# Lookup gates with one product per token: high and low part as 256 moving columns, added outside, rows accessed in pairs of words

## The chip, the cores and the metric

The kernel runs on one core of a Trainium2 chip. Its engines work side by side, each through its own queue of instructions: TensorE (PE, with its loads of the stationary operand shown as PEld), VectorE (DVE), ScalarE (ACT), GpSimd (POOL) and SyncE (SP), which issues the DMAs. The metric is the device time of one execution in microseconds; lower is better.

## What is computed

256 tokens of width 1024 pass two layers and then a second block (band attention, a recurrence, a mixture of experts, a gated output). Each of the two layers has a mixer and then this lookup of experts, and the change lies in the lookup alone:

```python
def peer(xn, w_q, sub_keys, u, v):          # 8 heads, 128 keys, 16 picks
    q = (t @ w_q).reshape(n_tok, PEER_HEADS, 2, PEER_DKEY // 2)
    sc = jnp.einsum('thpd,hpnd->thpn', q, sub_keys)
    s1, i1 = lax.top_k(sc[:, :, 0], PEER_TOPK)
    s2, i2 = lax.top_k(sc[:, :, 1], PEER_TOPK)
    cand = s1[..., :, None] + s2[..., None, :]     # of 256, the best 16
    cidx = i1[..., :, None] * PEER_NKEYS + i2[..., None, :]
    ...
    gate = jax.nn.softmax(top_s, axis=-1)
    hid = gelu(einsum('td,thkd->thk', tc, u[ec]))
    return einsum('thk,thkd->td', gc * hid, v[ec])
```

There are 128 x 128 = 16384 experts, and each token picks 8 x 16 = 128 of them.

## The kernel before

The kernel gathers no expert. It computes the hidden value of all 16384 experts for all 256 tokens and multiplies each by a gate, which is zero where the token did not pick that expert. The hidden values lie in `H`, by row: expert number = 128 * i1 + i2, `H` has i2 on its 128 partitions, and for each of the 128 rows i1 the 256 tokens side by side in float32. `H` is three tiles, `parts`: rows 0 to 63, 64 to 95, 96 to 127.

One layer of `peer` goes through these stages.

1. Queries (16 blocks) and the scores against the keys.
2. The row stage. For each row i1, `acc_t` (all its products carry the line of `mm`, L119) makes 24 products of 256 columns into the PSUM tile `ph`: 8 blocks of the width, each as high x high, low x high (alternating) and then 8 times high x low. The stationary operand is the row's weight block. It comes by DMA as `raw`, ACT casts its high part `whi`, DVE subtracts for the low part `wlo` (both L98). ACT takes the Gelu of `ph` (L771 for tokens whose gates are not yet in `H`, L774 for the others), and DVE multiplies the latter into the row (L775).
3. Beside the first 28 or so rows DVE chooses the experts (top 16, lookups). From then on, it also makes the gates, 4 tokens at a time in 64 groups, which `rate` spreads evenly over the remaining rows. `build` makes two one-hot tiles in float16: `pab` says at which of 128 places each of the 128 picks of a token has its i1 and its i2 (L735), `pgb` is the i2 half times the pick's gate (L738), once by the high and once by the low float16 part of the gate. `gates` sums over the picks on PE and lets the result meet `H`: rows that are already done (n of them) are multiplied on DVE (L755), the rows to come get the gate written into `H` by ACT (L758), and the Gelu is multiplied into it later.
4. The value stage, `acc`: rows of `H` in pairs are split into `hw`, ACT first and then DVE, and multiplied with the value weights by products of 512 columns. When a token half is finished, L824 adds it to `h`.

The gates of before are two products for each token, one by each part, which add up in PSUM:

```python
mm(ps[:, i * P:(i + 1) * P], b[:, part, :, i], ab[:, 0, :, i], part == 0, part == 1)
```

So 8 products of 128 columns for a group, each with its own stationary operand. In `pab` and `pgb` the 4 tokens lie side by side, so that one token's operand is one element in 4. The sum of a group is a PSUM bank of 512 words, [4 tokens][128 rows]. PSUM tiles of the small kind come from `smt` (4 buffers of one bank). `H` is accessed through `"p i t -> p t i"`: rows run fastest, which are 256 words apart, so no two words in a row of the access lie side by side.

Of the kernel before, what the change touches and what calls it, by code (L numbers as in the profile page):

```python
# [32 lines left out]
# pairs (a, b) of sorted candidates that can be among the best 16: first a, rows, columns  # L33
RECTS = ((0, 2, 16), (2, 2, 8), (4, 4, 4), (8, 8, 2))
NCAND = 80
# gates are held as two float16 parts of 2 ** 14 times their value
GATE_UNIT = 2.0 ** 14
# (1 + w) ** -0.5 - 1 as a polynomial in w, from the first power on
SQRT = (-0.49999831, 0.37499936, -0.3139437, 0.27433988)
NO_SYNC = mybir.DependencyInfo(mybir.DependencyClass.NoSync, mybir.DependencyReason.DATA)  # L40
# products of other work between two steps of the triangular inverses
PACE = 5
# pairs of expert rows for which the first token tile goes ahead of the second
TAIL = 2
# pieces of the first expert's weights split ahead of the choice of experts
EARLY = 2
# output gates of the recurrence that go ahead of the attention's projection
GATES = 0
REST = 2
# loads under way beside the usual ones while the experts' weights stream  # L50
# [3 lines left out]
def program(tc, A, out, stop=None, start=None):  # L54
# [18 lines left out]
    sm_ps = ctx.enter_context(tc.tile_pool(name="sm_ps", bufs=4, space=PSUM))  # L73
# [7 lines left out]
    def smt(nm="sm"):  # L81
        return sm_ps.tile([P, 512], F32, tag="sm", name=nm)
# [34 lines left out]
    def mm(o, l, r, start, stop):  # L117
        """a product; while paced, every few of them queue behind the next mark."""
        i = nc.tensor.matmul(o, l, r, start=start, stop=stop)  # L119
        per, n = paced  # L120
        if per and n // per < len(marks):
            tc.add_manual_dep(i.ins, marks[n // per].name, NO_SYNC, reason="pace")
            paced[1] += 1
        return i
# [6 lines left out]
    def acc_t(o, w, xT, base, nk, n=P):  # L131
        """o[n, t] = sum over nk blocks of w[:, base + k * P ...].T @ xT[:, k, :], high parts first."""
        for a, bs in ((0, (0, 1)), (1, (0,))):
            for k in range(nk):
                ws = w[a][:, base + k * P:base + k * P + n]
                for b in bs:
                    mm(o, ws, xT[b][:, k, :], a == 0 and b == 0 and k == 0, a == 1 and k == nk - 1)
# [20 lines left out]
    def rsqrt(r, v):  # L158
        """r = v ** -0.5: a first guess y from the exponent, then r = y * (1 + w) ** -0.5 with w = v * y ** 2 - 1,
        |w| < 0.07, whose polynomial is off by 2.4e-8 at most."""  # L160
# [37 lines left out]
    def to_T1(src, emit):  # L198
        """src[128, 1024] transposed block by block: emit(q, psum[128, 512]) for blocks 4 q to 4 q + 3."""
        for q in range(2):  # L200
            ps = smt("tp")
            for j in range(4):
                k = 4 * q + j
                nc.tensor.transpose(ps[:, j * P:(j + 1) * P], src[:, k * P:(k + 1) * P], ident)  # L204
            emit(q, ps.rearrange("p (k t) -> p k t", k=4))
# [7 lines left out]
    class Scratch:  # L213
        """room for a norm: half rows that come and go, and rows that stay."""
# [10 lines left out]
    class Rms:  # L225
        """rms norm of h with gain gi, token tile by token tile, into the transposed high and low parts."""
# [39 lines left out]
    class Unscaled(Rms):  # L266
        """the same without the token's scale, which late() returns beside it."""
# [16 lines left out]
    class Ln:  # L284
        """layer norm of the rows y, with the gain's and the bias's rows gb, into h and its transposed
        high and low parts, or to the output."""
# [40 lines left out]
    class Entry(Ln):  # L327
        """final rms norm of the first block and the layer norm that opens the second, in one."""
# [14 lines left out]
        def variance(self, t, v, var):  # L343
            # the rows lack the rms norm's scale, which divides the layer norm's epsilon instead
            q = tinyp.tile([P, 1], F32, tag="rv1", name="rv1")
            V.tensor_tensor(q, self.ss[:, t, 0:1], self.ss[:, t, 1:2], op=ALU.add)
            V.tensor_scalar(q, q, 1e-5 / D, 1e-11, op0=ALU.mult, op1=ALU.add)
            V.tensor_tensor(v, var, q, op=ALU.add)
# [10 lines left out]
    def fresh(make):  # L359
        """the norm of h as it stands."""  # L360
        with pool("fresh") as fp:
            nxt = make(Scratch(fp))
            for t in range(2):
                for n in range(2):
                    nxt.half(t, n)
            return nxt.late()

    def out_proj(wpool, src, xT, sink, order=(0, 1, 2, 3), both=1):
        """x @ w for w [1024, 1024], its granules in this order.
        After the first ones the first token tile goes ahead of the second."""  # L370
# [192 lines left out]
    def peer(l, xT, make):  # L563
        with ExitStack() as es:
# [10 lines left out]
            # routing scratch lies in the half of the hidden values that is written last  # L575
# [138 lines left out]

            w = wload(A["peer_w_q"][l, 0])
# [16 lines left out]
            def build(grp):  # L732
                ts = slice(4 * grp, 4 * grp + 4)
# [3 lines left out]
                b = pw.tile([P, 2, P, 4], F16, tag="pgb", name="pgb", bufs=2)  # L737
                V.tensor_tensor(b, ab[:, 1:2, :, :].to_broadcast([P, 2, P, 4]),  # L738
                                IT[:, 2:4, ts][:, :, None, :].to_broadcast([P, 2, P, 4]), op=ALU.mult)
                built[grp] = ab, b  # L740

            def gates(grp, n):
                t0 = 4 * grp
                ab, b = built.pop(grp)
                ps = smt("g")
                for i in range(4):
                    for part in range(2):
                        mm(ps[:, i * P:(i + 1) * P], b[:, part, :, i], ab[:, 0, :, i], part == 0, part == 1)
                pv = ps.rearrange("p (t i) -> p t i", t=4)
                for o, end, part in parts:  # L750
                    size = end - o
                    hv = part[:, :, t0:t0 + 4].rearrange("p i t -> p t i")
                    m = min(max(n - o, 0), size)
                    if m:
                        V.scalar_tensor_tensor(hv[:, :, :m], hv[:, :, :m], 1.0 / GATE_UNIT, pv[:, :, o:o + m],  # L755
                                               op0=ALU.mult, op1=ALU.mult)
                    if m < size:
                        ACT.activation(hv[:, :, m:], pv[:, :, o + m:end], AF.Copy, scale=1.0 / GATE_UNIT)  # L758
# [30 lines left out]
            while grp < 64:  # L789
                if grp not in built:  # L790
                    build(grp)
                gates(grp, NK)
                grp += 1
            acc = [[mmt(f"acc{t}{n}") for n in range(2)] for t in range(2)]
# [24 lines left out]
            # the last ones for the first token tile, then for the second  # L819
            for t in range(2):  # L820
                for n in range(2):
                    for i1, w, v in held:
                        value_block(i1, w, v, t, (n,))
                    V.tensor_tensor(h[:, t, half(n)], h[:, t, half(n)], acc[t][n], op=ALU.add)  # L824
# [16 lines left out]
    def residual(y, ln):  # L841
        """alpha * h plus a product, into the layer norm."""
# [8 lines left out]
    def band_mixer(xT):  # L851
        """alpha * x + mixed, then its layer norm."""
# [23 lines left out]
    def rwkv_and_band(xT, op, acc, sg):  # L876
        with ExitStack() as es:
# [23 lines left out]
            # pairwise products, transposed: [s, (ab, rb, ak, rk), t]  # L901
# [15 lines left out]
            # log decay, natural layout, then cumulated along time  # L917
# [34 lines left out]
            # normalised keys  # L952
# [26 lines left out]
            # scaled factors  # L979
# [52 lines left out]
            def invert():  # L1032
                """unit triangular inverses by block doubling."""
# [22 lines left out]
            # values in natural layout, bonus and output gate  # L1056
# [38 lines left out]
            def chunk(t):  # L1095
                """the recurrence over one half of the tokens."""
# [39 lines left out]
                # group norm  # L1136
# [58 lines left out]
    def band_attention(xT, oT, ep, ew):  # L1195
        """projects at once; returns what does the rest."""
# [10 lines left out]
        def core():  # L1207
            for side in range(2):
                b = 64 * side
                probs = []  # L1210
                for t in range(2):
                    n = P * (t + 1)
                    # the bias, then the scores with it, then their softmax
# [27 lines left out]
    def prepare():  # L1241
        """what the choice of experts and the ungated half of the last part need."""
# [6 lines left out]
        # sums the two parts of the logits and their bias  # L1249
# [8 lines left out]
    def parts_of_h(es):  # L1258
        """room for the high and low parts of h."""
# [3 lines left out]
    def moe(x):  # L1263
        xT, (carry, (rs, rb, iota1), products), xn = x
        pp = ctx.enter_context(pool("pp")).tile([P, 2, D], F32, tag="pp", name="pp")
        with ExitStack() as es:
# [30 lines left out]
            for t in range(2):  # L1297
                o = ps[:, S + t * 36:S + (t + 1) * 36]
                mm(o, lT[:73, tok(t)], rb[:73, :], True, True)
                # the group, and the token's place within it, counted from 1  # L1300
# [12 lines left out]
            # tokens gathered by group, transposed, and their weights  # L1313
# [11 lines left out]
            # group gate and the two best experts of the group  # L1325
# [32 lines left out]
            # loads land in their own room, and in that of the groups' sums while it is not needed  # L1358
# [59 lines left out]
            def overflow():  # L1418
                """the tokens past the first 128 of a group; no two groups can have such."""
# [48 lines left out]
            def weights():  # L1468
# [11 lines left out]
                # the largest group, should it have more than 128 tokens  # L1480
# [43 lines left out]
    def ple_products(ep):  # L1524
        """the ungated half of the last part: what it needs, then returns what does half n of it."""
# [33 lines left out]
    def after(name, x):  # L1559
        """what follows the named part, up to the part to stop at."""  # L1560
# [34 lines left out]
def gran_t(w, c0, n):  # L1595
    """[1024, ...] columns c0.. in n stationary granules [c][d part][dk, 128]."""
    w = w[:, c0:c0 + n * P].reshape(DK, P, n, P)
    return w.transpose(2, 1, 0, 3).reshape(n, P, 1024)


def gran_n(w, c0, n):
    """columns c0.. in n chunks of 512, each as granules [g][d part][2, 512]."""
# [112 lines left out]
```

## Time and profile before

| | |
|---|---|
| median of 3 runs | 2639.63 us (2638.01 to 2640.05) |
| the profiled execution, its span on the core | 2635.1 us |
| PE busy | 2556.6 us, 97% |
| loads of stationary operands busy | 2294.1 us, 87% |
| DVE busy | 1934.4 us, 73% |
| ACT busy | 1354.3 us, 51% |

The span runs from the first to the last instruction of the profiled execution; the page gives no other time for that execution, so the runs are read beside it. Busy means that an instruction was under way, and products overlap, so a product's duration is longer than what it adds; the distance from start to start is what it adds.

### The profile page before, as it was taken

What the parts mean: (1) busy time and instruction counts of PE and PEld (TensorE: products, weight loads), DVE (VectorE), ACT (ScalarE), POOL (GpSimd) and SP (SyncE); (2) the same over time, 40 slices, a digit from 0 to 9 for tenths busy, and PEclk for the clock granted to TensorE, in tenths of its full rate; (3) what the DMA queues carried; (4) which work ended last, traced back from release to release, by engine and by line L of the source; (5) the groups of instructions that cost most, each with busy time, mean ns of one, the idle gap of its engine ahead of it and who ended that gap; (6) DMA issues with size and microseconds to landing.
All of it is one profiled execution on the core that took longest, in us unless ns stands there. A gap on an engine that the chain in (4) does not pass through costs nothing. (4 is left out here: it accounts for less than half of the span.)

```text
span 2635.1 us, 42144 instructions
## 1 busy us (share of the span) xinstructions
PE 2556.6 (97%) x16202; PEld 2294.1 (87%) x16202; DVE 1934.4 (73%) x3547; ACT 1354.3 (51%) x2299; POOL 10.1 (0%) x25
## 2 busy tenths in 40 slices
PE   8999999999999999999999999999989999899996
PEld 7899999998888879899999998888878899788885
DVE  6689877887555566799778885555567466799997
ACT  5555655444444444555555444444455434478872
POOL 0000000000000000000000000000010000000000
PEclk9999999999999999999999999999989999899998
DMA  5445444444555554555444445555534214599983
GB/s 205 166 137 183 164 151 150 154 147 163 188 189 187 189 194 152 176 169 176 152 152 153 148 149 185 189 188 202 197 128 138 93 61 137 207 350 353 351 320 113
DMA packets 131777, 474.75 MB, mean 180 GB/s; under 512 B 15218, under 2 KB 16242, under 8 KB 131314
## 3 DMA queue, kind: packets, MB, share of 16 engines
q1 hardware_dynamic: 131570, 472.00, 52.3%
q8 instruction: 129, 2.11, 0.3%
q14 instruction: 78, 0.64, 0.1%
HBM read 470.89 MB, written 1.05 MB: 179 GB/s over the span
## 5 line engine op out<-in xcount | busy, mean ns | idle before, releaser
L98 DVE TENSOR_TENSOR wlo<-raw,whi 128x1024 fp32r<-128x1024 f32 x743 | 908.6, 1224 | 527.3 <-ACT whi L98 489.0
L98 ACT CAST whi<-raw 128x1024 fp32r<-128x1024 f32 x743 | 780.4, 1051 | 895.3 <-PE acc L119 357.1
L119 PE MATMUL ph<-xh,whi 128*128 128x256 f32 x2048 | 512.0, 288 | 0.0
L119 PE MATMUL acc<-whi,hw 128*128 128x512 f32 x1984 | 504.7, 396 | 2.5 <-ACT hw L98 2.2
L119 PE MATMUL ph<-xl,whi 128*128 128x256 f32 x2048 | 501.5, 283 | 0.0
L119 PEld LDWEIGHTS acc<-whi,hw 128*128 128x128 f32 x1984 | 373.7, 189 | 92.2 <-ACT hw L98 2.6
L119 PEld LDWEIGHTS ph<-xh,whi 128*128 128x128 f32 x2048 | 393.2, 192 | 0.1
L119 PEld LDWEIGHTS ph<-xl,whi 128*128 128x128 f32 x2048 | 392.4, 192 | 0.0
L119 PE MATMUL ph<-xh,wlo 128*128 128x256 f32 x2048 | 287.3, 283 | 0.0
L119 PE MATMUL acc<-wlo,hw 128*128 128x512 f32 x992 | 272.6, 396 | 0.0
L119 PEld LDWEIGHTS ph<-xh,wlo 128*128 128x128 f32 x2048 | 264.2, 192 | 0.0
L119 PEld LDWEIGHTS acc<-wlo,hw 128*128 128x128 f32 x992 | 187.1, 189 | 44.4
L119 PE MATMUL g<-pab,pgb 128*128 128x128 f16 x1024 | 140.7, 296 | 0.0
L98 DVE TENSOR_TENSOR mlo<-raw,mhi 128x1024 fp32r<-128x1024 f32 x96 | 116.7, 1223 | 10.9 <-ACT mhi L98 10.2
L755 DVE SCALAR_TENSOR_TENSOR H<-H,g 128x256 f32<-128x256 f32 (+26 forms) x254 | 121.1, 515 | 0.5 <-PE g L119 0.4
L758 ACT ACTIVATE H<-g 128x128 f32<-128x128 f32 (+20 forms) x254 | 67.8, 359 | 99.7 <-DVE H L755 99.7
L98 ACT CAST mhi<-raw 128x1024 fp32r<-128x1024 f32 x96 | 100.8, 1052 | 25.1 <-PE gu L119 19.4
L119 PEld LDWEIGHTS <-pgb 128*128 128x128 f16 x1024 | 105.0, 118 | 6.4
L738 DVE TENSOR_TENSOR pgb<-pab,IT 128x1024 f16<-128x1024 f16 x128 | 87.5, 688 | 1.9
L98 DVE TENSOR_TENSOR hw<-H,hw 128x512 fp32r<-128x512 f32 x128 | 87.2, 684 | 0.0
L735 DVE TENSOR_TENSOR pab<-iota,IT 128x1024 f16<-128x1024 f16 x128 | 87.1, 682 | 0.0
L771 ACT ACTIVATE H<-ph 128x256 f32<-128x256 f32 (+40 forms) x254 | 78.1, 307 | 12.0 <-PE ph L119 11.9
(655 smaller groups left out, 3591.9 us busy)
## 6 DMA issues: line engine op xcount, KB each, us to landing
raw<-in_peer_u SPq DMA_DIRECT2D x256, 512.0 KB, 3.2
raw<-in_peer_v SPq DMA_DIRECT2D x256, 512.0 KB, 3.9
raw<-in_exp_gu SPq DMA_DIRECT2D x128, 512.0 KB, 5.3
raw<-in_exp_down SPq DMA_DIRECT2D x64, 512.0 KB, 5.3
raw<-in_peer_w_q SPq DMA_DIRECT2D x32, 512.0 KB, 3.3
raw<-in_even_w_in SPq DMA_DIRECT2D x28, 512.0 KB, 4.2
raw<-in_odd_w_in SPq DMA_DIRECT2D x24, 512.0 KB, 3.8
raw<-in_w_in_g SPq DMA_DIRECT2D x16, 512.0 KB, 3.2
```

The source lines that it names most:

```text
L98: return ACT.copy(hi, src), V.tensor_tensor(lo, src, hi, op=ALU.subtract)
L119: i = nc.tensor.matmul(o, l, r, start=start, stop=stop)
L735: V.tensor_tensor(ab, iota4[:, None, :, :].to_broadcast([P, 2, P, 4]), IT[:, 0:2, ts][:, :, None, :].to_broadcast([P, 2, P, 4]), op=ALU.is ...
L738: V.tensor_tensor(b, ab[:, 1:2, :, :].to_broadcast([P, 2, P, 4]), IT[:, 2:4, ts][:, :, None, :].to_broadcast([P, 2, P, 4]), op=ALU.mult)
L755: V.scalar_tensor_tensor(hv[:, :, :m], hv[:, :, :m], 1.0 / GATE_UNIT, pv[:, :, o:o + m], op0=ALU.mult, op1=ALU.mult)
L758: ACT.activation(hv[:, :, m:], pv[:, :, o + m:end], AF.Copy, scale=1.0 / GATE_UNIT)
L771: ACT.activation(hrow[:, tk:], ph[:, tk:S], AF.Gelu)
```

## The change

The two parts of the gate change sides. `pgb` now holds the i1 half times the parts, and both parts of one token are the moving operand of one product, side by side as 256 columns; the stationary operand is the plain i2 half of `pab`. A group has 4 products instead of 8, and nothing adds up in PSUM: high and low sums lie apart, [high or low][128 rows] for each token, in a pair of banks (`pair`, 1024 words). A product writes every second word of half a bank pair: tokens 0 and 1 of a group are interleaved word by word in one bank, tokens 2 and 3 in the other.

ACT then copies the high sums into SBUF (`gs`), DVE adds the low ones for rows that are done and multiplies `H` by the sum, and for rows to come DVE writes high + low into `H`. `H`, the PSUM pair and `gs` are now accessed token pair by token pair, runs of 2 x 2 neighbouring words in `H`. The unit of the gates (2 to the 14th) is no longer taken out on the way into `H` but at the end, where a product of the value stage is added to `h`. While the queries and the rows run, the small PSUM tiles are 2 pairs of banks instead of 4 banks.

```diff
+    def use_small(wide):
+        if small[0]:
+            small[0].close()
+        small[0] = ExitStack()
+        small[1] = small[0].enter_context(tc.tile_pool(name="sw_ps" if wide else "sm_ps", bufs=2 if wide else 4,
+                                                       space=PSUM, reuse_waits="tile"))
+        small[2] = wide
...
     def smt(nm="sm"):
-        return sm_ps.tile([P, 512], F32, tag="sm", name=nm)
+        return small[1].tile([P, 512], F32, tag="sm", name=nm) if not small[2] else pair(nm)[:, :512]
+
+    def pair(nm):
+        return small[1].tile([P, 1024], F32, tag="sw", name=nm)
...
+            use_small(True)
             w = wload(A["peer_w_q"][l, 0])
...
-                b = pw.tile([P, 2, P, 4], F16, tag="pgb", name="pgb", bufs=2)
-                V.tensor_tensor(b, ab[:, 1:2, :, :].to_broadcast([P, 2, P, 4]),
+                g = pw.tile([P, 2, P, 4], F16, tag="pgb", name="pgb", bufs=2)
+                V.tensor_tensor(g, ab[:, 0:1, :, :].to_broadcast([P, 2, P, 4]),
                                 IT[:, 2:4, ts][:, :, None, :].to_broadcast([P, 2, P, 4]), op=ALU.mult)
-                built[grp] = ab, b
+                built[grp] = ab, g
...
-                ps = smt("g")
+                ps = pair("g")
+                pv = ps.rearrange("p (b r i t) -> p b r i t", b=2, r=2, t=2)
                 for i in range(4):
-                    for part in range(2):
-                        mm(ps[:, i * P:(i + 1) * P], b[:, part, :, i], ab[:, 0, :, i], part == 0, part == 1)
-                pv = ps.rearrange("p (t i) -> p t i", t=4)
+                    mm(pv[:, i // 2, :, :, i % 2], ab[:, 1, :, i], g[:, :, :, i], True, True)
+                hi, lo = [pv[:, :, r, :, :].rearrange("p b i t -> p i b t") for r in range(2)]
+                sums = pw.tile([P, 512], F32, tag="pw", name="gs").rearrange("p (i b t) -> p i b t", b=2, t=2)
+                ACT.copy(sums, hi)
+
+                def add(o, a, b):
+                    V.tensor_tensor(o, lo[:, a:b], sums[:, a:b], op=ALU.add)
+
+                add(sums[:, :n], 0, n)
                 for o, end, part in parts:
-                    size = end - o
-                    hv = part[:, :, t0:t0 + 4].rearrange("p i t -> p t i")
-                    m = min(max(n - o, 0), size)
-                    if m:
-                        V.scalar_tensor_tensor(hv[:, :, :m], hv[:, :, :m], 1.0 / GATE_UNIT, pv[:, :, o:o + m],
-                                               op0=ALU.mult, op1=ALU.mult)
-                    if m < size:
-                        ACT.activation(hv[:, :, m:], pv[:, :, o + m:end], AF.Copy, scale=1.0 / GATE_UNIT)
+                    hv = part[:, :, t0:t0 + 4].rearrange("p i (b t) -> p i b t", b=2)
+                    m = min(max(n, o), end)
+                    if m > o:
+                        V.tensor_tensor(hv[:, :m - o], hv[:, :m - o], sums[:, o:m], op=ALU.mult)
+                    if m < end:
+                        add(hv[:, m - o:], m, end)
...
                 gates(grp, NK)
                 grp += 1
+            use_small(False)
...
-                    V.tensor_tensor(h[:, t, half(n)], h[:, t, half(n)], acc[t][n], op=ALU.add)
+                    V.scalar_tensor_tensor(h[:, t, half(n)], acc[t][n], 1.0 / GATE_UNIT, h[:, t, half(n)],
+                                           op0=ALU.mult, op1=ALU.add)
```

The rest of the diff takes out comments and docstrings, which moves line numbers: L98, L119, L735, L738, L755, L775 and L824 of before are L113, L134, L753, L756, L781, L800 and L850 after; L771 and L774 after are the copy of the high sums and the additions of the low ones.

On DVE, the first layer's row stage where 58 rows are done, before (`wlo` is the low part of the next row's weights, `ge` the Gelu that is multiplied into a row):

```order
L98 TENSOR_TENSOR wlo<-raw,whi 128x1024
L735 TENSOR_TENSOR pab<-iota_1365,IT 128x1024
L755 SCALAR_TENSOR_TENSOR H<-H,g 128x4x58
L775 TENSOR_TENSOR H<-H,ge 128x68
L738 TENSOR_TENSOR pgb<-pab,IT 128x1024
L98 TENSOR_TENSOR wlo<-raw,whi 128x1024
```

The same place on DVE after the change:

```order
L113 TENSOR_TENSOR wlo<-raw,whi 128x1024
L753 TENSOR_TENSOR pab<-iota_1365,IT 128x1024
L800 TENSOR_TENSOR H<-H,ge 128x68
L774 TENSOR_TENSOR gs<-g,gs 128x232
L774 TENSOR_TENSOR H<-g,gs 128x6x4
L774 TENSOR_TENSOR H<-g,gs 128x32x4 x2
L756 TENSOR_TENSOR pgb<-pab,IT 128x1024
L781 TENSOR_TENSOR H<-H,gs 128x58x4
L113 TENSOR_TENSOR wlo<-raw,whi 128x1024
```

Between two `wlo` there is now one multiplication without the scalar in place of the scaled one, and four additions (the sums of the rows done, and three for the rows to come, which were ACT's).

On PE, the last products of the first layer's row stage before (the group of gates here is the last one, and 24 products of `ph` for the last row stand between it and the first `acc` of the value stage; of the 16 alternating ones the last four are shown):

```order
L119 MATMUL ph<-xh,whi 128x256
L119 MATMUL ph<-xl,whi 128x256
L119 MATMUL ph<-xh,whi 128x256
L119 MATMUL ph<-xl,whi 128x256
L119 MATMUL ph<-xh,wlo 128x256 x8
L119 MATMUL acc_7732<-whi,hw 128x512
```

And after, from the last group's first load on:

```order
L134 LDWEIGHTS pab
L134 MATMUL g<-pgb,pab 128x256
L134 LDWEIGHTS pab
L134 MATMUL g<-pgb,pab 128x256
L134 LDWEIGHTS pab
L134 MATMUL g<-pgb,pab 128x256
L134 LDWEIGHTS pab
L134 MATMUL g<-pgb,pab 128x256
L134 MATMUL ph<-xh,wlo 128x256 x8
L134 MATMUL acc_7676<-whi,hw 128x512
```

The last group has moved behind the 16 alternating products of the last row, and 8 products are left between it and the value stage.

## Rows read from the trace of the kernel before

**Rows 1.** The page of the profile: its first line and busy time of each engine.

```profile
span 2635.1 us, 42144 instructions
PE 2556.6 (97%) x16202; PEld 2294.1 (87%) x16202; DVE 1934.4 (73%) x3547; ACT 1354.3 (51%) x2299; POOL 10.1 (0%) x25
```

**Rows 2.** Stretches: us; busy us of PE, PEld, DVE, ACT, POOL; clock; DMA; GB/s.

```profile
300.00:400.00 100.00, 100.00 (x839) 99.04 (x838) 77.88 (x133) 53.01 (x147) 0.00 (x0) 1.00 0.44 150
500.00:600.00 100.00, 100.00 (x840) 98.98 (x840) 86.25 (x149) 42.34 (x106) 0.00 (x0) 1.00 0.44 149
```

**Rows 3.** Waits of PE from 300 to 640 us: the only row.

```profile
PE acc L119 <- ACT hw L98: 1.1, 1, 1.1
```

**Rows 4.** Costliest groups: busy us, mean ns | idle before; the gates over both layers.

```profile
L119 PE MATMUL g<-pab,pgb 128*128 128x128 f16 x1024 | 140.7, 296 | 0.0
L119 PEld LDWEIGHTS <-pgb 128*128 128x128 f16 x1024 | 105.0, 118 | 6.4
L755 DVE SCALAR_TENSOR_TENSOR H<-H,g 128x256 f32<-128x256 f32 (+26 forms) x254 | 121.1, 515 | 0.5 <-PE g L119 0.4
L758 ACT ACTIVATE H<-g 128x128 f32<-128x128 f32 (+20 forms) x254 | 67.8, 359 | 99.7 <-DVE H L755 99.7
```

**Rows 5.** Timeline of PE and PEld around one group, start us, duration us.

```profile
402.03 0.28 PE L119 MATMUL ph<-xl,whi 128*128 128x256 f32 x1
402.04 0.19 PEld L119 LDWEIGHTS ph<-xh,whi 128*128 128x128 f32 x1
...
403.82 1.12 PE L119 MATMUL ph<-xh,wlo 128*128 128x256 f32 x8
404.78 0.11 PEld L119 LDWEIGHTS <-pgb 128*128 128x128 f16 x1
404.78 1.11 PE L119 MATMUL g<-pab,pgb 128*128 128x128 f16 x8
404.88 0.42 PE L119 MATMUL g<-pab,pgb 128*128 128x128 f16 x2
405.01 0.12 PEld L119 LDWEIGHTS <-pgb 128*128 128x128 f16 x1
405.01 0.41 PE L119 MATMUL g<-pab,pgb 128*128 128x128 f16 x2
...
405.64 0.37 PE L119 MATMUL ph<-xh,whi 128*128 128x256 f32 x1
405.85 0.28 PE L119 MATMUL ph<-xl,whi 128*128 128x256 f32 x1
```

**Rows 6.** Timeline of PE, two other places, products of 256 and 128 columns.

```profile
1969.11 1.89 PE L119 MATMUL cum<-tri,u 128*128 128x256 f32 x8
...
2064.11 0.72 PE L119 MATMUL i<-XT,it 128*128 128x128 f32 x5
```

**Rows 7.** Timeline and forms of DVE in the row stage, one to a row.

```profile
L755 DVE SCALAR_TENSOR_TENSOR H<-H,g 128x256 f32<-128x256 f32 x42 | 31.3, 745 | 0.0
L755 DVE SCALAR_TENSOR_TENSOR H<-H,g 128x128 f32<-128x128 f32 x22 | 9.5, 433 | 0.2 <-PE g L119 0.2
L775 DVE TENSOR_TENSOR H<-H,ge 128x240 f32<-128x240 f32 x2 | 0.8, 397 | 0.0
L775 DVE TENSOR_TENSOR H<-H,ge 128x128 f32<-128x128 f32 x2 | 0.6, 284 | 0.0
...
562.78 1.22 DVE L98 TENSOR_TENSOR wlo<-raw,whi 128x1024 fp32r<-128x1024 f32 x1
563.92 0.37 DVE L775 TENSOR_TENSOR H<-H,ge 128x208 f32<-128x208 f32 x1
```

**Rows 8.** Forms of ACT, 300 to 640 us: a copy of 512 words.

```profile
L98 ACT CAST hw<-H 128x512 fp32r<-128x512 f32 x4 | 2.4, 619 | 0.0
```

**Rows 9.** Timeline at the end of the first row stage.

```profile
624.46 1.12 PE L119 MATMUL ph<-xh,wlo 128*128 128x256 f32 x8
...
626.65 2.07 PE L119 MATMUL acc<-whi,hw 128*128 128x512 f32 x6 [1.08 <-ACT hw L98]
```

More of the change, by code (lines that the diff above doesn't have):

```diff
@@ L72, in program @@
     mm_ps = ctx.enter_context(tc.tile_pool(name="mm_ps", bufs=2, space=PSUM))
-    sm_ps = ctx.enter_context(tc.tile_pool(name="sm_ps", bufs=4, space=PSUM))
+    small = [None, None, False]
+    def use_small(wide):
[6 more added lines that the diff above has]
+    use_small(False)
+    ctx.callback(lambda: small[0].close())
     banks = [0]
@@ L742, in gates @@
             def gates(grp, n):
                 t0 = 4 * grp
-                ab, b = built.pop(grp)
-                ps = smt("g")
+                ab, g = built.pop(grp)
+                ps = pair("g")
+                pv = ps.rearrange("p (b r i t) -> p b r i t", b=2, r=2, t=2)
                 for i in range(4):
-                    for part in range(2):
-                        mm(ps[:, i * P:(i + 1) * P], b[:, part, :, i], ab[:, 0, :, i], part == 0, part == 1)
-                pv = ps.rearrange("p (t i) -> p t i", t=4)
@@ L793, in peer @@
                 grp += 1
+            use_small(False)
             acc = [[mmt(f"acc{t}{n}") for n in range(2)] for t in range(2)]
```

## The prediction

> **What bounds the kernel now.** I read the page first, then the windows of the row stage, then the waits of PE there, then single products in the timeline. The page [rows 1] has PE busy for 2556.6 of 2635.1 us. The windows [rows 2] sharpen that for the stage the change lies in: PE is busy for all of each 100 us at full granted clock (0.99 to 1.00, the 2.4 GHz level), DVE for 78 to 86 us, ACT for 42 to 53. The waits [rows 3] confirm it: from 300 to 640 us PE waits once, 1.1 us, at the start of the value stage; the second layer's row stage answers the same. So in the row stage time is what PE's products take, one behind the other, and whatever is taken off them comes off the span as long as DVE keeps up.
>
> Two distances are needed. Eight `ph` products of 256 columns end 1.12 us after the first starts, one alone lasts 0.28 [rows 5]: (1.12 - 0.28) / 7 = 0.120 us from start to start. The eight gate products of 128 columns last 1.11 us, one alone 0.296 [rows 4, 5]: (1.11 - 0.296) / 7 = 0.116. Half the columns cost as much. The whole group delays the next row: the second `ph` behind it starts at 405.85 [rows 5]; without the group it would have started two slots after the last `wlo` product's slot began at 404.66, at 404.90. A group costs 0.95 us of PE, 128 groups 121.6 us.
>
> Why 0.116? An ordinary load begins as the product before it starts (402.03 and 402.04, [rows 5]) and disappears behind it. The first gate load doesn't: it begins at 404.78, when the last `ph` has streamed, not a slot earlier. And the next row's first product is issued 0.047 us after the last gate product (405.64 against about 405.595), as if 128 columns streamed in some 0.05. I read this as load and stream one after the other, 0.066 + 0.05 (the first load of a group less, 0.05, since the second product comes 0.10 after it, at 404.88). It is a reading, and the rivals below are the others.
>
> **The change, part by part.**
>
> *Products.* Eight of 128 columns become four of 256, all with a load of the same form (float16, one element in 4). The columns stay 1024, four loads go. A stream of 256 columns lies between 2 x 0.048 = 0.096 and the whole `ph` slot, 0.120; I take 0.107. First product 0.05 + 0.107, three more at 0.066 + 0.107, and 0.02 until the next row's load has caught up: 0.70 us for 0.95. That is -0.25 a group, -31.5 us in 128 groups. If the load hides, the slot is 0.12 (the lower bound); if the product streams at half rate it is 0.215 or more, the distance of eight 256-column products elsewhere, (1.89 - 0.38) / 7 [rows 6], with their own loads behind them.
>
> *Writes to every second word.* The new products write each second word of a bank. No product of the trace is known to do so, so its price lies between nothing and that half rate. I take nothing: the only slow 256-column row is of another stage and shows no such access. The Trainium skill, PSUM — Partial Sum Buffer, section Specifications (TRN2), speaks against the change here: it gives lines of 8 bytes and says that any access that isn't contiguous slows products significantly. By it every column would fill a line of its own. No run here shows it yet; what it would make of the time is rival C.
>
> *DVE.* Before, a group cost 121.1 / 128 = 0.95 us [rows 4]. A scaled multiplication costs 745 ns for 256 words, 433 for 128 [rows 7], 2.44 ns a word; a plain one 397 for 240 and 284 for 128, 1.01 ns a word and 155 ns beside, of which some 80 overlap with the neighbour (1.22 us lasts the one at 562.78, and the next starts at 563.92). After, a group is an addition over 4n words, additions of 512 - 4n words into `H` and multiplications of 4n: 512 + 4n words in about five instructions. The rows done average about 79, so 828 x 1.01 + 5 x 75 = 1.21 us, +0.27. There are 0.65 groups to a row, and a row lasts about 3.45 us now. In the window from 300 us (n around 40) a group rises from about 0.5 to 1.05: 78% of 3.45 = 2.69 us a row become 3.05. In the last window (n around 110) it stays at about 1.35, since the cheaper words pay for the more: 2.98. Rows shrink by 0.65 x 0.25 = 0.16 to 3.29 us. So DVE stands at 91 to 93% of it: covered, but nearly without reserve. That cover is what rival D takes away. If every access cost the 2.44 ns a word of L755, a group would be 2.0 + 0.4 = 2.4 us at n = 79; this and 1.21 are its bounds, and I take the plain multiplication, since the accesses become runs of neighbouring words.
>
> *ACT.* It loses 67.8 / 128 = 0.53 us of writing gates a group and gets a copy of 512 words, 0.62 [rows 8]. At 42 to 53 us in 100 that is covered by PE's rows. It also loses the wait behind DVE, 99.7 us over the kernel [rows 4], which cost nothing.
>
> *Waits of PE.* The pairs of banks are two, not four. A group's products come 5 us apart and its copy and additions are about 2 us behind, so a second pair is always free. The scores before the row stage need 256 columns each and one ACT copy; nothing.
>
> *End of the row stage.* The new order of instructions has 8 products between the last group and `acc`, where there were 24. Eight are 0.96 us. In the shadow must now lie: the copy (0.62), the additions (0.60 + 0.08), the multiplications that still stand ahead in DVE's queue (0.34 + 0.21 + 0.20 + 0.34) and the one into the first rows (0.34), then ACT's first cast of `hw` (0.62): 3.35 us. PE waits 2.4 instead of 1.08 (the wait that [rows 9] carry, with eight products of 1.12 us ahead of it): +1.3 a layer, +2.6 us.
>
> *The unit.* Four scaled additions a layer in place of four plain ones, of 512 words. By [rows 7] one costs at most 4 x 0.149 = 0.6 us more, and only a layer's last has no products of PE beside it: 1.2 us at most, and I take nothing.
>
> Sum: -31.5 + 2.6 = -28.9 us, a span of 2606.2. The runs' median stands 4.5 us above the profiled span, so **2611 us**.
>
> **The rivals.**
>
> B. *The load hides behind the longer stream.* For it: from the second gate product on, the load does start with the product before it (405.01 and 405.01, [rows 5]); and five float32 products of 128 columns elsewhere are (0.72 - 0.276) / 4 = 0.111 apart [rows 6], as far as the gates', with loads that do hide at 256. Against it: the first gate load, which waited. Slots of 0.12: 0.05 + 4 x 0.12 = 0.53, -0.42 a group, -53 + 2.6: 2589 us. The Trainium skill, TensorE: Matmul & The Clock Gate, section Step-by-step: what each phase is for, has the next load run during this product; by that rule it would be B, and the first load of a group here disagrees.
>
> C. *The other side: writes at half rate.* For it: a product with 256 columns can take 0.215 [rows 6]; against it: nothing in this trace says that the words' distance did that. Stream 0.215 and load 0.066 apart make 0.28 a product, 1.11 in all: +0.163 a group, +21 + 2.6: 2664 us. It decides as soon as a product's distance is above 0.95 / 4 = 0.237.
>
> E. *Nothing is gained: columns are what a group costs.* Either the writes run at half rate and the load hides behind them (4 x 0.215 + 0.08 = 0.94), or the float16 operand with its 8-byte steps was always read at half rate (128 columns in 0.107, the load hidden), and twice the columns take twice that. For it: the sameness of 0.116 and 0.120. Against the second: the 0.047 above. About -1 + 2.6: 2641 us. This is also the case that the change doesn't do what it says.
>
> D. *DVE becomes the bound.* A row has 2.83 us of DVE now, the mean of the windows, 0.62 of it for gates. If only the additions that read PSUM (512 words) cost 2.44 ns a word, a group takes 1.21 + 512 x 1.43 = 1.94 us and a row 2.83 - 0.62 + 1.26 = 3.47: 98 rows x 0.02 x 2 layers + 2.6 = +7, 2646 us. It decides from 3.29 us a row on, 1.66 us a group, and is even with today at 1.9. With all words so, 2.4 us a group make 3.77 a row, +63 (counted in F). For it: L755 read PSUM at 2.44 ns a word; against: L755 also stepped 256 words through `H`, which the change takes away.
>
> F. More than C (writes and DVE's accesses slow), above 2667.
>
> **How the numbers follow.** The reading of the load is mine against two plausible others, and the write price is open. A (as forecast) 0.33, with 2600 to 2620 as its own range; B 0.20; C 0.18; E 0.14; D 0.10; F 0.05. The likeliest is A: 2611. From B's value to C's, 2588 to 2667, leaves out F and the tails of the others. A measurement tells no difference within 0.2%, 2634.4 to 2644.9. Faster are A and B: 0.53; within 0.2% most of E and a little of D: 0.14; slower C, F and the rest of D: 0.33.
>
> **What would show it.** In the changed trace: the distance of two gate products, 0.17 (A), 0.12 (B), 0.28 (C), 0.22 (E). PE's waits in the row stage: none, or DVE's `wlo` in D. DVE's busy share there, 91 to 93%, and the additions of `gs` at about 1 ns a word. A row of 3.3 us. The wait of `acc` on ACT's `hw`, about 2.4 us. The forecast is wrong if the distance is not 0.17, or if PE starts to wait for `wlo`.

## The result, and the profile after

The changed kernel takes 2660.41 us (median of 4 runs, 2658.36 to 2663.74) against 2638.82 us of the kernel before beside it. The ratio is 1.0078 (95% interval 1.0066 to 1.0090): 0.8% slower. The forecast was 2611, faster.

The page of the changed kernel, first line, busy times and the groups of the gates (busy, mean ns of one | idle before), answers to [rows 1, 4]:

```profile
span 2656.5 us, 41598 instructions
...
PE 2565.2 (97%) x15690; PEld 2258.2 (85%) x15690; DVE 1976.7 (74%) x3929; ACT 1373.4 (52%) x2173; POOL 10.1 (0%) x25
...
L134 PE MATMUL g<-pgb,pab 128*128 128x256 f16 x512 | 142.2, 412 | 3.9 <-DVE pgb L756 3.9
...
L771 ACT COPY gs<-g 128x512 f32<-128x512 f32 x128 | 75.5, 590 | 63.4 <-PE g L134 54.1
```

Half as many gate products take as much of PE as before (142.2 us for 140.7). The timeline of PE around one group, as in [rows 5]:

```profile
406.46 1.09 PE L134 MATMUL g<-pgb,pab 128*128 128x256 f16 x4
407.18 0.48 PE L134 MATMUL ph<-xh,whi 128*128 128x256 f32 x1
407.50 0.28 PE L134 MATMUL ph<-xl,whi 128*128 128x256 f32 x1
```

Four products, one of them 0.412 us, last 1.09: (1.09 - 0.412) / 3 = 0.226 us from start to start; the median of all starts in the trace is 0.229. A group delays the second `ph` behind it by 0.929 us, where it was 0.950 (medians of the groups). So the change gains 0.021 us x 128 = 2.7 us on PE, not 31.5. The span grew by 21.4, and the waits of PE from 300 to 640 us (waited for: us in total, times, longest) begin to say where. Before, [rows 3], there was one row of 1.1:

```profile
PE acc L134 <- ACT hw L113: 4.4, 1, 4.4
PE ph L134 <- ACT ge L799: 2.5, 1, 2.5
PE g L134 <- DVE pgb L756: 2.0, 1, 2.0
```

Three waits, one each; the second layer has the same three (4.4, 1.9 and 1.7). The windows (columns as in [rows 2]) show the first of the two stretches of a stage that are not full (the second, its end, stands further down), and small ones what follows it:

```profile
300.00:400.00 100.00, 96.23 (x707) 88.75 (x707) 83.30 (x204) 49.46 (x104) 0.00 (x0) 0.97 0.44 142
400.00:500.00 100.00, 100.00 (x768) 93.22 (x766) 84.95 (x188) 51.17 (x107) 0.00 (x0) 1.00 0.47 150
500.00:600.00 100.00, 100.00 (x768) 93.33 (x767) 88.08 (x183) 50.47 (x104) 0.00 (x0) 1.00 0.47 149
...
302.00:304.00 2.00, 0.40 (x2) 0.00 (x0) 2.00 (x5) 0.59 (x1) 0.00 (x0) 0.80 0.69 219
304.00:306.00 2.00, 1.14 (x5) 1.14 (x6) 2.00 (x10) 0.79 (x4) 0.00 (x0) 0.50 0.54 207
306.00:308.00 2.00, 2.00 (x11) 2.00 (x11) 0.08 (x2) 0.00 (x0) 0.00 (x0) 0.50 0.01 2
308.00:310.00 2.00, 2.00 (x12) 2.00 (x11) 0.00 (x0) 1.04 (x1) 0.00 (x0) 0.50 0.00 0
310.00:312.00 2.00, 2.00 (x15) 1.65 (x14) 1.36 (x3) 0.59 (x1) 0.00 (x0) 1.00 0.00 0
```

From 400 us on PE is full at full clock and DVE keeps up at 85 to 88%. But at the first group PE stands idle twice, and then the granted clock is 0.50, the 1.2 GHz level, until about 310 us: products come at half pace though PE is busy. The timelines of PE and ACT there, start and duration, with the idle time ahead:

```profile
299.06 0.30 PE L699 MATMUL it<-ident,H 128*128 128x128 f32 x1 [0.19 <-DVE H L692]
301.31 1.09 PE L134 MATMUL g<-pgb,pab 128*128 128x256 f16 x4 [1.95 <-DVE pgb L756]
302.44 0.59 ACT L771 COPY gs<-g 128x512 f32<-128x512 f32 x1 [3.44 <-PE g L134]
304.36 0.38 ACT L796 ACTIVATE H<-ph 128x252 f32<-128x252 f32 x1 [1.34 <-DVE H L774]
304.86 0.58 PE L134 MATMUL ph<-xh,whi 128*128 128x256 f32 x1 [2.46 <-ACT ge L799]
```

The first group stands right behind the transpose `it`, with no row's product between, so PE waits for DVE to build it. ACT's copy of its sums stands ahead of the Gelus of finished rows, and the first of these Gelus then waits another 1.34 us for DVE's additions of the same group (L774). PE waits again until a Gelu frees a `ph` bank. Before, 2.5 us of row products lay between `it` and the first groups (two of them, 16 products):

```profile
303.36 0.27 PE L684 MATMUL it<-ident,H 128*128 128x128 f32 x1
303.39 0.36 PE L119 MATMUL ph<-xh,whi 128*128 128x256 f32 x1
...
305.87 2.05 PE L119 MATMUL g<-pab,pgb 128*128 128x128 f16 x16
```

The end of the stage, answering to [rows 9]:

```profile
629.01 1.32 PE L134 MATMUL ph<-xh,wlo 128*128 128x256 f32 x8
...
629.77 0.58 ACT L771 COPY gs<-g 128x512 f32<-128x512 f32 x1
...
630.68 1.21 DVE L113 TENSOR_TENSOR wlo<-raw,whi 128x1024 fp32r<-128x1024 f32 x1
631.81 0.68 DVE L774 TENSOR_TENSOR gs<-g,gs 128x508 f32<-128x508 f32 x1
...
632.48 0.81 DVE L781 TENSOR_TENSOR H<-H,gs 128x256 f32<-128x256 f32 x3
...
634.04 1.14 ACT L113 CAST hw<-H 128x512 fp32r<-128x512 f32 x2 [3.28 <-DVE H L781]
...
634.71 2.93 PE L134 MATMUL acc<-whi,hw 128*128 128x512 f32 x6 [4.37 <-ACT hw L113]
```

The account of +21.4 us: groups -2.7; waits in the two row stages 8.9 + 8.0 for 1.1 + 1.1 before (the second layer's rows are 4.4, 1.9 and 1.7), +14.7. What is left, +9.4, fits the half clock, which stands behind the start and the end of both row stages (the second layer's are the rows from 1262 us on):

```profile
304.00:310.00 6.00, 5.14 (x24) 5.14 (x25) 2.08 (x10) 1.83 (x5) 0.00 (x0) 0.50 0.18 70
634.00:638.00 4.00, 3.29 (x8) 2.65 (x9) 1.98 (x5) 1.14 (x2) 0.00 (x0) 0.57 0.18 74
1262.00:1264.00 2.00, 1.48 (x4) 0.58 (x4) 2.00 (x3) 0.00 (x0) 0.00 (x0) 0.58 0.83 252
1264.00:1270.00 6.00, 4.33 (x22) 3.91 (x22) 3.31 (x13) 1.68 (x6) 0.00 (x0) 0.57 0.30 91
1594.00:1600.00 6.00, 5.00 (x12) 3.95 (x13) 2.27 (x6) 1.47 (x3) 0.00 (x0) 0.50 0.16 61
```

PE's busy time in each, times the share of the clock that is missing, adds up to 9.0 us. That is an estimate from these rows.

### The profile page after: what moved, and what is told of

Same layout as the page of the kernel before. It is cut to its first block, busy times and chain, and to the rows that moved or that the text cites. A ratio compares the mean times of both kernels' runs of the same rounds, so it can differ in the third digit from the quotient of the medians.

```text
span 2656.5 us, 41598 instructions
## 1 busy us (share of the span) xinstructions
PE 2565.2 (97%) x15690; PEld 2258.2 (85%) x15690; DVE 1976.7 (74%) x3929; ACT 1373.4 (52%) x2173; POOL 10.1 (0%) x25
## 5 line engine op out<-in xcount | busy, mean ns | idle before, releaser
L113 DVE TENSOR_TENSOR wlo<-raw,whi 128x1024 fp32r<-128x1024 f32 x743 | 908.5, 1224 | 484.2 <-ACT whi L113 435.2
L113 ACT CAST whi<-raw 128x1024 fp32r<-128x1024 f32 x743 | 780.3, 1051 | 844.1 <-PE acc L134 360.1
L134 PE MATMUL ph<-xh,whi 128*128 128x256 f32 x2048 | 523.2, 292 | 4.1 <-ACT ge L799 4.1
L134 PE MATMUL acc<-whi,hw 128*128 128x512 f32 x1984 | 507.0, 397 | 8.7 <-ACT hw L113 8.7
L134 PE MATMUL ph<-xl,whi 128*128 128x256 f32 x2048 | 508.0, 285 | 0.0
L134 PEld LDWEIGHTS acc<-whi,hw 128*128 128x128 f32 x1984 | 374.8, 189 | 99.5 <-ACT hw L113 9.2
L134 PEld LDWEIGHTS ph<-xh,whi 128*128 128x128 f32 x2048 | 394.9, 193 | 16.2 <-ACT ge L799 5.9
L134 PEld LDWEIGHTS ph<-xl,whi 128*128 128x128 f32 x2048 | 395.1, 193 | 3.5
L134 PE MATMUL ph<-xh,wlo 128*128 128x256 f32 x2048 | 295.7, 286 | 0.0
L134 PE MATMUL acc<-wlo,hw 128*128 128x512 f32 x992 | 273.2, 396 | 0.0
L134 PEld LDWEIGHTS ph<-xh,wlo 128*128 128x128 f32 x2048 | 268.7, 192 | 3.3
L134 PEld LDWEIGHTS acc<-wlo,hw 128*128 128x128 f32 x992 | 187.3, 189 | 45.3
L134 PE MATMUL g<-pgb,pab 128*128 128x256 f16 x512 | 142.2, 412 | 3.9 <-DVE pgb L756 3.9
L113 DVE TENSOR_TENSOR mlo<-raw,mhi 128x1024 fp32r<-128x1024 f32 x96 | 116.8, 1223 | 10.8 <-ACT mhi L113 10.2
L113 ACT CAST mhi<-raw 128x1024 fp32r<-128x1024 f32 x96 | 100.9, 1053 | 25.0 <-PE gu L134 19.0
L771 ACT COPY gs<-g 128x512 f32<-128x512 f32 x128 | 75.5, 590 | 63.4 <-PE g L134 54.1
L753 DVE TENSOR_TENSOR pab<-iota,IT 128x1024 f16<-128x1024 f16 x128 | 87.7, 686 | 14.1 <-PE g L134 13.7
L756 DVE TENSOR_TENSOR pgb<-pab,IT 128x1024 f16<-128x1024 f16 x128 | 87.3, 682 | 0.0
L113 DVE TENSOR_TENSOR hw<-H,hw 128x512 fp32r<-128x512 f32 x128 | 87.3, 684 | 0.0
L113 ACT CAST hw<-H 128x512 fp32r<-128x512 f32 x128 | 78.5, 616 | 6.6 <-DVE H L781 6.6
L134 PEld LDWEIGHTS <-pab 128*128 128x128 f16 x512 | 49.6, 122 | 32.6 <-DVE pgb L756 4.3
```

The lines of the kernel that those rows point to most:

```text
L113: return ACT.copy(hi, src), V.tensor_tensor(lo, src, hi, op=ALU.subtract)
L753: V.tensor_tensor(ab, iota4[:, None, :, :].to_broadcast([P, 2, P, 4]), IT[:, 0:2, ts][:, :, None, :].to_broadcast([P, 2, P, 4]), op=ALU.is ...
L756: V.tensor_tensor(g, ab[:, 0:1, :, :].to_broadcast([P, 2, P, 4]), IT[:, 2:4, ts][:, :, None, :].to_broadcast([P, 2, P, 4]), op=ALU.mult)
L771: ACT.copy(sums, hi)
```

## The experiments

Theories on the product: writes to every second word run at half rate (W); the moving operand's steps are read at half rate (R); later, the 16-bit type (T) against the step (D). On the rest of the loss: the two ends of the row stage, against DVE's work all along.

**Dense writes.** 

> The changed kernel, but each gate product writes 256 neighbouring words of PSUM (token by token, high then low part); ACT and DVE step through PSUM instead. In the changed kernel two gate products are 0.229 us apart. Theory W (writing every second word halves the rate): 0.12 here with the load hidden, 0.17 with load and stream one after the other; a group falls from 0.93 to about 0.53 or 0.70 us, and the time by 128 times that, from 2660 to about 2609 or 2631. Theory R (the moving float16 operand, one element in 4, is read at half rate): the distance stays at 0.22 to 0.23 and the time at 2660.

```diff
-ps.rearrange("p (b r i t) -> p b r i t", b=2, r=2, t=2)
+ps.rearrange("p (b t r i) -> p b t r i", b=2, t=2, r=2)
```

2659.86 us, products 0.229 apart: no change. Taken alone this spoke for R. One group of it:

```profile
408.70 1.09 PE L134 MATMUL g<-pgb,pab 128*128 128x256 f16 x4
```

**Dense moving operand.** 

> The changed kernel, but the moving operand lies token by token, so a product reads 256 neighbouring float16 elements; the writes still go to every second word. Theory R: products 0.12 us apart. Theory W: 0.229 as in the changed kernel. DVE writes this operand with wide steps now, so its 0.68 us may grow; the distance of the products decides, not the time.

```diff
-g = pw.tile([P, 2, P, 4], F16, ...)
+g = pw.tile([P, 4, 2, P], F16, ...)
-V.tensor_tensor(g, ...)
+V.tensor_tensor(g.rearrange("p t r i -> p r i t"), ...)
```

Products are 0.216 apart at full clock: neither theory as it stood. Time 3064.08 us, since DVE took 4.85 us for each `pgb` instead of 0.68, and PE waited for it 253.6 us. One group on PE, and the group of the line of `pgb`:

```profile
416.15 1.06 PE L134 MATMUL g<-pgb,pab 128*128 128x256 f16 x4
...
L756 DVE TENSOR_TENSOR pgb<-pab,IT 128x1024 f16<-128x1024 f16 x128 | 621.0, 4852 | 0.0
```

**Before, with writes apart.** 

> The kernel before, but its 8 products of 128 columns write every fourth word of the bank (the 4 tokens interleaved). Before they are 0.116 to 0.118 us apart. If writes apart run at half rate (W) and load and stream follow one another: 0.066 + 0.107 = 0.17. W with a hidden load, or theory R: no change, 0.118.

```diff
-mm(ps[:, i * P:(i + 1) * P], b[:, part, :, i], ...)
+mm(ps[:, i::4], b[:, part, :, i], ...)
```

0.118 apart, 2634.01 us in its one run: no change, as R or a masked W would have it.

**Gates off both ends.** 

> The changed kernel, but the first group of gates comes two rows later and the last group about four rows before the end of the row stage. In the changed kernel PE waits 2.0 us for the first pgb and 2.5 us for a Gelu at the first group, 4.4 us at the first value product, in each layer, and the granted clock falls to 0.50 for some microseconds behind both. Theory: these places are all of the loss, since a group itself costs 0.93 us against 0.95; without them the time is 2636 to 2642. Rival: DVE's extra work costs time all along the row stage; then it stays above 2650.

```diff
-rate = 64.0 / (NK - 2 - i1)
+rate, due = (64.0 + 2.0) / (NK - 7 - i1), -2.0
```

2638.30 us, ratio to before 1.0001 (0.9991 to 1.0011). The theory holds: the products and DVE's extra work are those of the changed kernel, and the whole loss stood at the two ends. PE's waits from 195 to 640 us, and the window of the first groups:

```profile
PE acc L134 <- ACT hw L113: 1.0, 1, 1.0
PE ph L134 <- ACT ge L799: 0.9, 1, 0.9
PE acc L134 <- DVE hw L113: 0.7, 1, 0.7
```

```profile
300.00:310.00 10.00, 10.00 (x79) 9.30 (x78) 9.29 (x19) 4.08 (x6) 0.00 (x0) 1.00 0.48 158
```

**Only the end.** 

> The changed kernel, with only the last groups four rows earlier; the first group stays where it is. With both moved it was 2638.3. Theory: the end's wait (4.4 us for 1.1) with its stretch at half clock is 5 us a layer, the start's (2.0 and 2.5 us, then 7 us at half clock) 6 us a layer; so 2660 - 10 = 2650. Rival: one of the two places is all of it: 2638 or 2660.

 (the rate's divisor is `NK - 6 - i1`, `due` starts at 0.) 2657.88 us, ratio 1.0069 (1.0043 to 1.0095): a miss. The wait of `acc` fell to 1.3 us, but the quicker pace brought two more waits around 310 us (0.8 for `IT`, and 0.9 more for a Gelu). So moving the end alone gains next to nothing; how the 21 us split between the ends stays open.

**bfloat16.** 

> The changed kernel with bfloat16 in place of float16 in the one-hot tiles and the gates, same shapes and steps (the low part of a gate is coarser than in the reference's terms, so the sums are less exact). Theory T (a 16-bit float16 operand streams at 2 columns in the time of 4-byte ones' 4): if it is float16 alone, the distance falls from 0.229 to 0.12; if all 16-bit operands, or the width of the step, it stays at 0.21 to 0.23.

 0.229 apart, 2665.27 us in one run: not float16 alone.

**Half the stationary columns.** 

> The changed kernel with each gate product cut in two, 64 stationary columns each (the load of 64 columns has another form than that of 128), 8 products of 256 columns a group. If the form of the 128-column float16 load is what slows the stream, a product of 256 columns takes 0.12 us here and a group 0.96 us; if float16 columns themselves cost 0.87 ns each, a product stays at 0.22 to 0.23, a group takes 1.85 us and the time is about 2660 + 128 x 0.92 = 2778.

 2696.24 us in one run. Two products on different halves of the columns start within 0.01 us of each other and run side by side; a pair takes 0.228, a group 1.24 us and not 1.85. That is neither forecast. A load of another form leaves the distance, which speaks against the load.

**fp32r, dense.** From here on the writes are dense and the gates off both ends, unless said. 

> The changed kernel with dense writes and the gates moved off both ends of the row stage (which together stood at 2638), and with both operands of the gate products turned into fp32r by two ACT casts (512 and 1024 words a group), token by token. So far float16 and bfloat16 products of 256 columns were 0.216 to 0.229 us apart whatever was dense, and the rows' fp32r products 0.120. Theory T (the operand's type sets the pace, two cycles a 16-bit column): 0.12 here, a group 0.5 us for 0.93, and 2638 - 128 x 0.42 = 2585 if ACT keeps up (about 2.8 us of a row of 3.2). Rival (the gate products are slow for another reason, such as starting each sum anew): 0.22 still, 2640 or more.

```diff
+aR = pw.tile([P, 4, P], F32R, ...)
+gR = pw.tile([P, 4, 2, P], F32R, ...)
+ACT.copy(aR, ab[:, 1].rearrange("p i t -> p t i"))
+ACT.copy(gR.rearrange("p t r i -> p t (r i)"), g.rearrange("p r i t -> p t (r i)"))
...
-mm(..., ab[:, 1, :, i], g[:, :, :, i], True, True)
+mm(..., aR[:, i], gR[:, i], True, True)
```

(Here the pool `pw` has 3 buffers instead of 4, for room.) 0.119 apart, a group 0.47 us. 2628.77 us, ratio 0.9954 (0.9936 to 0.9972): faster than both, but 44 us above the expectation; PE waits 27.5 us for `pgR`.

**fp32r, apart.** 

> The same, but both fp32r operands lie with the four tokens side by side, so a product reads one word in 4. If steps cost nothing: 0.12 as in the dense one. If wide steps halve the rate: 0.22.

 0.235 to 0.237 apart, 2694.31 us in one run: the same type, half the pace. So the step alone can halve it; whether a 16-bit type would do so too, this run can't tell. One group:

```profile
407.17 1.20 PE L134 MATMUL g<-pgR,paR 128*128 128x256 f32 x4
```

**fp32r written by DVE.** 

> The same, but DVE writes the moving operand as fp32r itself (one word in 4, no ACT cast for it); ACT casts the stationary one. DVE's pgb grows from 0.68 to about 1.1 us if the wider output is slower. Products 0.12 apart by theory T; time 2585 if DVE keeps up, 2600 to 2620 if DVE, at 3.0 + 0.65 x 0.4 = 3.26 us a row, becomes the bound.

 0.213 to 0.233 apart (stationary dense, moving apart), `pgb` 1.22 us, 2738.70 us, ratio 1.0377 (1.0359 to 1.0396): worse than its worst case, since the products did not get faster either.

**float16, dense.** 

> As the dense fp32r kernel (dense writes, gates off both ends of the row stage, operands repacked token by token by two ACT copies), but the repacked operands stay float16. Theory T (the 16-bit type costs two cycles a column): products 0.22 apart, group 0.93, time 2640 or more. Theory D (it is the step between elements, of either operand, that costs the second cycle: fp32r one word in 4 was 0.235 as well): 0.12 apart, a group about 0.5, time about 2629 or less as in the dense fp32r one (2628.8).

 (`F32R` becomes `F16` in the lines above, `pw` has its 4 buffers.) 0.109 apart, a group 0.45 us, 2599.06 us; ratio 0.9856 (0.9839 to 0.9872). T has fallen, as D forecast, and this version beats both kernels by more than 1%. Of the 61 us that 0.48 us less a group make, 39 arrive against the kernel with the gates off both ends (2638.30): PE now waits 11.4 us for `pgR` and 7.7 for Gelus.

**float16, only the stationary operand dense.** 

> The same, but only the stationary operand is repacked; the moving one is read one element in 4. With the stationary one apart and the moving one dense a product took 0.216, with both apart 0.229. Theory D: about 0.21 to 0.23 here too, the moving operand alone sets it. If only the stationary operand's step cost: 0.12.

 0.228 apart, a group 0.91, 2651.62 us in one run: the moving operand's step alone is enough. No run has the stationary operand alone apart; with the writes apart as well, it makes no difference (0.216 in the dense-moving run, 0.215 in the next).

**float16, dense, with writes apart.** 

> As the dense float16 kernel, but the products write every second word of PSUM, as in the changed kernel. So far that cost nothing where the operands already set 0.229. If writes apart run at half rate by themselves, 0.21 to 0.23 here against the dense one's distance; else the same distance as there.

 0.215 apart, a group 0.87, 2647.34 us in one run: the writes alone are enough, too. The three in PE's timeline, one group each and the row's product behind it (dense, then still dense, then spread):

```profile
406.42 0.61 PE L134 MATMUL g<-pgR,paR 128*128 128x256 f16 x4
406.78 0.36 PE L134 MATMUL ph<-xh,whi 128*128 128x256 f32 x1
```

```profile
409.77 1.07 PE L134 MATMUL g<-pgb,paR 128*128 128x256 f16 x4
410.48 0.48 PE L134 MATMUL ph<-xl,whi 128*128 128x256 f32 x1
```

```profile
411.13 1.04 PE L134 MATMUL g<-pgR,paR 128*128 128x256 f16 x4
411.81 0.47 PE L134 MATMUL ph<-xh,wlo 128*128 128x256 f32 x1
```

From the first gate product to the row's product: 0.36, 0.71 and 0.68 us (0.72 in the changed kernel). So one step of either kind halves the pace, and both together cost no more than one: that is why each of the first experiments, which took away one, showed next to nothing.

**Dense, built by DVE.** 

> The dense float16 kernel without its two ACT copies: DVE builds both one-hot tiles token by token itself, the pick's number or gate now the operand that repeats for 128 neighbouring elements. Products 0.11 apart as in the dense kernel (2599). If DVE keeps its 0.68 us for 1024 elements in this order, ACT is relieved of 1.8 us a group, PE's waits for the repacked operand (11 us) go, and the time is 2585 to 2595. If the repeating operand costs DVE its pace (1.1 to 1.2 us each, +0.65 us a row that has 93% of DVE busy), DVE bounds the rows: 2680 or more.

```diff
-V.tensor_tensor(ab, iota4[:, None, :, :]..., IT[:, 0:2, ts][:, :, None, :].to_broadcast([P, 2, P, 4]), ...)
+V.tensor_tensor(ab, iota4[:, None, :, :]..., IT[:, 0:2, ts][:, :, :, None].to_broadcast([P, 2, 4, P]), ...)
```

2684.58 us, ratio 1.0178 (1.0160 to 1.0196): the bad case. The products stay at 0.109, but DVE takes 1.215 us for each tile and is the bound; a window and the line of `pab`:

```profile
400.00:500.00 100.00, 89.97 (x717) 85.06 (x716) 100.00 (x187) 48.67 (x100) 0.00 (x0) 0.98 0.43 138
```

```profile
L753 DVE TENSOR_TENSOR pab<-iota,IT 128x1024 f16<-128x1024 f16 x128 | 155.4, 1215 | 0.2
```

## Why the prediction was wrong

**Products (-31.5, measured -2.7).** The step that failed is "load and stream one after the other, 0.066 + 0.05", with 0.107 for a stream of 256 columns, 0.173 a product. The runs show 0.229: the load is hidden (0.228 with the stationary operand dense too), and the stream runs at half rate, because the moving operand is one element in 4; with everything dense it is 0.109. Half of 0.228 is 0.114, so a stream at half rate accounts for nearly all of the 0.118 of before's 128 columns. That is worked out, not run: no run has the operands of before dense, and its loads, 118 ns each [rows 4], may be a second limit of the same size.

Two signs misled me. The 0.047 us to the next row's product, read as the time of the stream, does not measure the columns: the still-dense kernel has 0.046 there with 256 columns, the dense one 0.028, the spread one 0.070. And the first load of a group begins 0.12 us after the start of the last row product in the dense kernel too (406.41 against 406.30), where products are 0.109 apart, so it does not show that loads cost time.

Rival E had named both causes, the reading at half rate and the writes with the load hidden, and gave 2641; with the ends mended the kernel stands at 2638. I gave it 0.14. That the time lies within my range, near rival C's 2664, is luck: C's 0.28 a product did not come. The 0.215 that I took from [rows 6] for half rate fits by luck as well: those products (`cum`) have plain float32 operands, dense on all sides. (And 0.25 x 128 is 32.0, not the sum's 31.5, which changes nothing.)

**Writes to every second word (nothing taken).** Wrong as a price, without effect here: alone they raise 0.109 to 0.216, in the change they hide behind the moving operand's step. The Trainium skill's sentence in PSUM — Partial Sum Buffer, Specifications (TRN2), agrees with these two numbers. On the other side, the Trainium skill, SBUF — State Buffer, section Specifications (TRN2), has lines of 16 bytes that give full rate from two hits a line. The trace differs: float16 elements 8 bytes apart, two to a line, read at half rate (0.228 against 0.109), little better than fp32r words 16 bytes apart (0.233 where only the moving operand lay so).

**Waits of PE (nothing taken).** Wrong: the two waits at the first group are 8.1 us in the two layers, with a half clock behind them. I had priced the buffers and the middle of the stage, and read the new order at its end but not at the first group, where it has the four products right behind `it`, and ACT's copy and DVE's additions ahead of the next Gelu.

**End of the stage (2.4 us, measured 4.4).** The terms were right (copy 0.58, addition 0.68), but a Gelu of 0.38 us stands ahead of the copy and a `wlo` of 1.21 ahead of the additions. No term had the half clock behind an idle PE, which the table of before could not show in this stage.

**DVE (+0.27 a group, covered).** Right: DVE's busy time rose by 42.3 us, 0.33 a group, and PE never waited for `wlo` in the row stages. The two forms that matter, from 300 to 620 us: 419 ns for 256 words, and 658 for the 480 words of an addition that reads PSUM. DVE was busy 85 to 88% in the full windows, where 91 to 93% had counted on shorter rows; rival D did not come.

```profile
L781 DVE TENSOR_TENSOR H<-H,gs 128x256 f32<-128x256 f32 x39 | 16.3, 419 | 0.0
...
L774 DVE TENSOR_TENSOR gs<-g,gs 128x480 f32<-128x480 f32 x1 | 0.7, 658 | 0.0
```

**ACT, the unit.** ACT's copy took 0.59 us and ACT stayed at about 50%: right. The scaled additions (L850) take 682 ns for 512 words, the plain ones of before (L824) 679: nothing, as taken. They read PSUM as well, so neither the scalar nor PSUM by itself made the 2.44 ns a word of L755; its step of 256 words through `H` is what is left, which no run tested alone.

## What to carry to other kernels

A product's pace is set by its slowest stream: ask separately whether the moving operand and the output are dense, and change both, since here mending one of two equal limits showed nothing. When a new order of instructions is at hand, read it where a stage begins as well as where it ends: an instruction that waits holds back all that stand behind it on its queue, and a TensorE that stood idle (here 4.4 us at the end of a stage) can run on at half clock, 0.50 here. Repacking on an engine with room (ACT here) can be worth it: 1.8 us of ACT a group bought 0.48 us of PE, the bound, and 1.4% of the kernel.

## What was not expected of the hardware

A spread output costs DVE much: 4.85 us for 1024 float16 elements each written 512 bytes behind the last, against 0.68 side by side; and 1.215 us where one operand repeats for 128 neighbouring elements. Two products with 64 stationary columns each, on different halves, run side by side, a pair in 0.228 us. At half clock a dense row product comes every 0.213 us instead of 0.120, and a gate product of the changed kernel (first group of the second layer) every 0.427 instead of 0.229.
